# Attention scores that contract over all 128 rows, and value panels at twelve places

## The chip, the cores and the metric

The kernel runs on one core of a Trainium2 chip. The metric is the device time of one execution in microseconds (us). Engines are named as in the profile: PE is TensorE (matrix products; PEld are its weight loads), DVE is VectorE, ACT is ScalarE, POOL is GpSimd, SP is SyncE, which issues most transfers. TensorE takes a stationary operand (the weights, loaded first) and streams a moving operand; both have the contracted dimension on the partitions, of which there are 128.

## The reference, cut to what matters

Two transformer-like blocks, one after the other, each of two layers, on 256 tokens of width 1024. The first block also carries 256 context tokens. In each of its layers there are a feed-forward net, a mixing stage and another feed-forward net; the mixing stage has four branches: a Fourier mix, a neighbourhood attention (4 heads of 64), a gated linear attention, and a grouped-query attention (4 query heads on 2 key heads of 64). The second block has a latent attention (8 heads of 96), a differential attention, a memory attention and a squared-ReLU net. The scores that the change touches are these:

```
# neighbourhood attention: per head, 64 contracted channels, keys of the grid and of the context
s = concat([einsum(q, k_window) * scale + bias, einsum(q, k_ctx) * scale]);  p = softmax(s)
# grouped-query attention: two query heads share one key head
s = einsum('bqhgd,bkhd->bhgqk', q_blk, k);  p = softmax(s);  o = einsum(p, v)
# differential attention: two score maps of 64 channels for each head
o = softmax(q1 @ k1.T) @ v - lambda * softmax(q2 @ k2.T) @ v
```

## The kernel before, in words

Everything is kept with channels on the partitions and tokens along the rows of memory. A linear layer takes a weight panel of 1024 x 256 in two loads of 512 KB (`raw_panel`, line 118 on), splits each into a high and a low part of a shorter f32 format (`split`: ScalarE line 133, VectorE line 134) and forms three products for each 128 contracted channels (`mm3`). All products are issued in `mm`, line 84, so the profile shows that line for all of them and tells them apart by their tiles. In `lin_T` the panel is the stationary operand and the activations move; in `lin_tok` (line 190) it is the other way round: the panel moves. That form makes the values of the attentions: `gvt` and `nvt` in the first block, `dv` (line 1281) and the memory values (`mem_values`, line 303) in the second.

A split panel lies in a tile of 2112 words, and `off` (line 145) says at which word it begins; the low part follows 1024 words later. The panels of dv and of the memory values use `MOVING2 = 0`.

Scores are made by `scores` (line 249): products into a bank of TensorE's output memory, the row maximum (line 268), the exponential with its sum (line 272); `weights` divides by the sum and `transposed` (line 280) turns the weights for the product with the values.

In the neighbourhood attention (`na`, line 831) two heads lie in one tile, 64 channels each on partitions 0 to 63 and 64 to 127. A score product takes the 64 partitions of its head from the query tile `nq` and from the key tile `nk`. The grouped attention (`gqa`, line 910) does the same with the tile `gqt`, whose third part holds both key heads. These products are in full f32, which the trace shows as two passes for each. Keys and queries are normalized by `headnorm` (line 566): a copy out of the bank, a square, a product with a block matrix that gives the mean of each head's squares, and a scaling; `later` puts the second half of that behind the next product.

In the differential attention (`prepare`, line 1289, and `attend`, line 1362) each head pair has a query tile `a` (trace: `qs`) and a key tile `b_` (`ks`) of 128 partitions. For the map c, partitions of map c hold the high part of query and key, the other 64 the low part of the query beside a copy of the high part of the key. One product over 128 partitions so gives high x high and low x high. The tile `lk` holds the low part of the keys, and a second product, over the 64 partitions of map c alone, adds high x low:

```
scores([((a[:, c, j, w], b_[:, c, j]), (a[64 * c:64 * c + 64, c, j, w], lk[64 * c:64 * c + 64, j]))
        for j in range(2)], mp, after=after) for c in range(2)
```

`prepare` makes these tiles for one pair of heads with ScalarE (line 1297), VectorE (line 1298) and transfers on SP's queue (line 1302); it is called one pair ahead.

The order of the work is set in three ways. The calls give a program order; a planner then orders the instructions of each engine by that order and by when it expects their inputs, before the kernel runs; and `behind` adds edges by hand. In the mixing stage the branches are generators called in `ORDER` (line 44). In the differential attention `FILL` (line 60) says how many pieces of gate and merge products stand before and after the scores of each of the eight units (one unit is one pair of heads and 128 queries).

Of the kernel before, what the change touches and what calls it, by code (L numbers as in the profile page):

```python
# [13 lines left out]
F32 = mybir.dt.float32  # L14
# [63 lines left out]
def _build(ctx, nc, tc, A, out, tap, upto):  # L78
# [63 lines left out]

    WIDE, NARROW, MOVING, MOVING2 = 8, 24, 36, 0
    LATE = 28

    def panel(*srcs, off=WIDE):
# [153 lines left out]

    def mem_values(l, M, t0, dst):
        for c in range(2):
            pn = panel(A["mem_w_kv_2"][l][:, 512 + c * 256:768 + c * 256], off=MOVING2)
            ps = PM("pmv")
            for tb in range(2):
                lin_tok(ps[:, tb * 256:tb * 256 + 256], pn, cols(0, 256), M, t0 + tb * P)
            act(out=r2(dst).rearrange("p (t c) n -> p t c n", c=2)[:, :, c], in_=r2(ps), func=AF.Copy)
# [73 lines left out]

    slab = lambda name, dt=F32: mp.tile([P, 512], dt, name=name, tag="slab", bufs=10)
    gslab = lambda name, dt=F32: mp.tile([P, 512], dt, name=name, tag="gslab", bufs=10)
    tmp = lambda name="t": mp.tile([P, 512], F32, name=name, tag="tmp", bufs=3)

    def mixing_constants(after):
# [174 lines left out]
                    norm if g1 == NFF else None, side)  # L563


    def headnorm(raw, n, gain, dst, tiles=None, tag="po"):


        if raw is not None:
            act(out=dst, in_=raw, func=AF.Copy)  # L570
        sq, *tiles = tiles or [tmp("sqh"), *rs_tiles(mp)]
        sq = sq[:, :n]
        act(out=sq, in_=dst, func=AF.Square)

        def rest():
            pq = PM("phn", tag)
            after = newest[0]
            behind(mm(pq[:, :n], C["b64"], sq, start=True, stop=True), after)
            y = rstd(pq[:, :n], tiles)
            V.scalar_tensor_tensor(out=dst, in0=dst, scalar=gain, in1=y, op0=ALU.mult, op1=ALU.mult)  # L580
        return rest

    def mixing(l, H, first, last, side=None):
        W = A["w_in"][l]
# [215 lines left out]
        def na_in():  # L800

            pan = wpan("na_q")
            nq, nk = [], []
            for j in range(2):
                ps = PM("pnq")
                lin_T(ps[:, :nT], pan, cols(j * P, j * P + P), H, 0, nT)
                o = slab("nq")
                later(headnorm(ps[:, :nT], nT, gv[:, l, 0:1], o[:, :nT]))
                nq.append(o)
            yield  # L810
            pan = wpan("na_k")
            for j in range(2):
                ps = PM("pnk")
                lin_T(ps, pan, cols(j * P, j * P + P), H, 0, 512)
                o = slab("nk")
                later(headnorm(ps, 512, gv[:, l, 1:2], o))
                nk.append(o)
            yield
            pan = wpan("na_v")
            nvt = []  # L820
            for t in range(2):
                ps = PM("pnv")
                for b in range(2):
                    lin_tok(ps[:, b * 256:(b + 1) * 256], pan, cols(0, 256), H, (2 * t + b) * P)
                    later()
                o = slab("nvt")
                act(out=o, in_=ps, func=AF.Copy)
                nvt.append(o)
            T.nq, T.nk, T.na_v = nq, nk, lambda b, h: nvt[b // 2][:, (b % 2) * 256 + 64 * h:(b % 2) * 256 + 64 * h + 64]

        def na():

            nq, nk, na_v = T.nq, T.nk, T.na_v
            new_out(slab, 2, 3)
            for hp in range(2):
                bts = []
                for j in range(2):
                    bt = mp.tile([P, 512], F32, name="rpb", tag="rpb", bufs=2)
                    behind(nc.sync.dma_start(out=bt.rearrange("p (b k) -> p b k", b=2), in_=A["rpb"][l, 2 * hp + j]),
                           loaded[-1])  # L840
                    bts.append(bt)
                for qb in range(2):
                    w = slice(qb * P, qb * P + P)
                    pts = []
                    for j in range(2):
                        r = slice(64 * j, 64 * j + 64)
                        pts.append(weights([(nq[hp][r, w], nk[hp][r, :])], mp, bts[j][:, qb * 256:(qb + 1) * 256]))
                    po = PM("po", "po")[:, :P]
                    for b in range(4):
                        for j in range(2):  # L850
                            ins = mm(po[64 * j:64 * j + 64], na_v(b, 2 * hp + j), pts[j][:, b * P:(b + 1) * P], start=b == 0,
                                     stop=b == 3)
                    flow.append(ins)
                    put(2 + hp, w, po)
                    yield
            for qb in range(2 if zq else 0):
                w = slice(256 + qb * P, 256 + qb * P + P)
                pts = []
                for j in range(2):
                    r = slice(64 * j, 64 * j + 64)  # L860
                    pts.append(weights([(nq[c][r, w], nk[c][r, 256:]) for c in range(2)], mp))
                po = PM("po", "po")[:, :256]
                for c in range(2):
                    for b in range(2):
                        for j in range(2):
                            ins = mm(po[64 * j:64 * j + 64, c * P:c * P + P], na_v(2 + b, 2 * c + j),
                                     pts[j][:, (2 * c + b) * P:(2 * c + b + 1) * P], start=b == 0, stop=b == 1)
                flow.append(ins)
                for c in range(2):
                    put(2 + c, w, po[:, c * P:c * P + P])  # L870
                yield

        def gqa_in():

            gqt = mp.tile([P, 3, 512], F32, name="gqt", tag="gqt", bufs=1)
            pan = panel(A["w_gq"][l], off=NARROW if last else WIDE)
            for j in range(2):
                ps = PM("pqq")
# [4 lines left out]
            ps = PM("pqk")  # L883
            lin_T(ps, pan, cols(0, P), H, 0, 512)
            headnorm(ps, 512, gv[:, l, 3:4], gqt[:, 2, :])()
            ps = PM("pqv")
            lin_T(ps, pan, cols(P, 2 * P), H, 0, 512)
            later()
# [9 lines left out]
            for c, m in ((0, 2), (2, 1)):  # L898
# [6 lines left out]
                V.tensor_tensor(out=rot, in0=rot, in1=bc(ax[:, 256:]), op=ALU.mult)  # L905
                V.tensor_tensor(out=g, in0=g, in1=bc(ax[:, :256]), op=ALU.mult)
                V.tensor_tensor(out=g, in0=g, in1=rot, op=ALU.add)
            T.gqt, T.qv = gqt, qv

        def gqa():  # L910

            gqt, qv = T.gqt, T.qv
            new_out(slab, 6, 7)
            for kv in range(2):
                r = slice(64 * kv, 64 * kv + 64)
                for z in range(2 if zq else 1):
                    for qb in range(2):
                        w = slice(256 * z + qb * P, 256 * z + qb * P + P)
                        if z == 0:
                            pts = [weights([(gqt[r, c, w], gqt[r, 2, :])], mp) for c in range(2)]  # L920
                            at = lambda c, b: pts[c][:, b * P:(b + 1) * P]
                        else:
                            pt = weights([(gqt[r, c, w], gqt[r, 2, 256:]) for c in range(2)], mp)
                            at = lambda c, b: pt[:, (2 * c + b) * P:(2 * c + b + 1) * P]
                        po = PM("po", "po")[:, :P]
                        nb = 4 - 2 * z
# [120 lines left out]
    def _block2(c2):  # L1047
# [9 lines left out]
        x2 = lambda dp: x_all[:, 2 * dp:2 * dp + 2]  # L1057
        mean = {n: mp.tile([P, P], F32, name=f"mean{n}") for n in (384, 256)}
        mean[128] = C["b64"]
        for n, t in mean.items():  # L1060
            V.memset(t, 1.0 / n)

# [115 lines left out]
        for l in range(DEPTH):  # L1178
# [99 lines left out]
                    nc.gpsimd.dma_start(out=rotz[a:a + 8], in_=t[b:b + 8])  # L1278
                rope(t, rotz, cd, sd, slice(0, P), 8)
            for c in range(4):  # L1280
                pn = panel(W[:, OFF2["dv"] + 256 * c:OFF2["dv"] + 256 * c + 256], off=MOVING2)
                ps = PM("pdv")
                for tb in range(2):
                    lin_tok(ps[:, tb * 256:tb * 256 + 256], pn, cols(0, 256), X, tb * P)
# [4 lines left out]
            def prepare(hp):  # L1289
# [1 line left out]

                hs = slice(2 * hp, 2 * hp + 2)
                a, b_ = (med(n, F32R).rearrange("p (c h t) -> p c h t", c=2, h=2) for n in ("qs", "ks"))
                lk = mp.tile([P, 2, 256], F32R, name="lk", tag="lk", bufs=2)
                lq = r2(mp.tile([P, 512], F32R, name="lq", tag="tmp", bufs=5))
                for t, src, lo in ((b_, dk, lk), (a, dq, lq)):
                    act(out=t, in_=src[:, hs].unsqueeze(1).to_broadcast([P, 2, 2, 256]), func=AF.Copy)
                    V.tensor_tensor(out=lo, in0=src[:, hs], in1=t[:, 0].bitcast(F32), op=ALU.subtract)
                    for c in range(2):
                        own, other = (slice(64 * i, 64 * i + 64) for i in (c, 1 - c))  # L1300
                        part = t[own, c] if src is dk else lo[own]
                        nc.sync.dma_start(out=t[other, c].bitcast(F32), in_=part.bitcast(F32))
                return a, b_, lk
# [58 lines left out]
            def attend(u, after=None):  # L1362

                hp, qb = divmod(u, 2)
                if qb == 0 and hp < 3:
# [1 line left out]
                a, b_, lk = ready[hp]  # L1367
                w = slice(qb * P, qb * P + P)
                (p0, r0, _), (p1, r1, _) = (
                    scores([((a[:, c, j, w], b_[:, c, j]), (a[64 * c:64 * c + 64, c, j, w], lk[64 * c:64 * c + 64, j]))  # L1370
                            for j in range(2)], mp, after=after) for c in range(2))
                for j in range(2):
                    u, v_ = p0[:, 256 * j:256 * j + 256], p1[:, 256 * j:256 * j + 256]
# [352 lines left out]
```

## Time and profile before

| | us |
|---|---|
| median of 3 runs | 2816.1 (2815.95 to 2817.97) |
| the profiled execution | 2818.12 |
| its span, first to last instruction | 2816.3 |
| TensorE busy | 2766.3 |
| VectorE busy | 1930.4 |
| ScalarE busy | 1322.4 |
| GpSimd busy | 81.7 |

The span is what the trace covers; the profiled execution's own time is 1.8 us longer. Busy time of TensorE is the union of its matmuls' bars. The bars overlap, because matmuls are pipelined, so the distance from one start to the next says how long one takes in a stream, not the length of the bar. A row of the timeline merges equal neighbours: "x24" are 24 instructions, the second number is the time from the start of the first to the end of the last. "64*128" in a matmul's row are the contracted rows and the columns of its weights.

### The profile page before, as it was taken

Reading aid. Unit: us, or ns where it says so; the run is one execution under the profiler, and the core shown is the slowest. Engines: PE = TensorE matmul, PEld = TensorE weight load, DVE = VectorE, ACT = ScalarE, POOL = GpSimd, SP = SyncE. Lnnn points to the kernel's source line nnn. Section 1 sums busy time; section 2 is a strip of 40 time slices with the busy share of each in tenths; the row PEclk is TensorE's granted clock in tenths of the full one; section 3 lists DMA queues with packets and bytes.
Section 4 is the critical chain, followed back from the end, with each engine's and each line's share of the span. In section 5 each row is a group of like instructions: output and inputs, shape, how many; then the busy total and the mean of one; then the engine's idle time right before and its main releaser. Section 6 shows DMA issues by size and latency. Waiting matters only on the chain.

```text
span 2816.3 us, 45494 instructions
## 1 busy us (share of the span) xinstructions
PE 2766.3 (98%) x18310; PEld 2422.0 (86%) x18310; DVE 1930.4 (69%) x3049; ACT 1322.4 (47%) x2102; POOL 81.7 (3%) x93
## 2 busy tenths in 40 slices
PE   7999999999999999999999999999999999999998
PEld 4888887669888898888877999999899999999898
DVE  4978565856767568883568766576686576757766
ACT  5222245654323243232457644556755456566554
POOL 0000000000000000000000000000110011001100
PEclk9999999999999999999999999999999999999999
DMA  7766433114555436653333566647456655554564
GB/s 250 230 188 201 138 96 90 29 46 127 183 154 187 134 124 191 199 182 94 96 90 87 154 193 185 174 117 189 134 168 209 193 162 139 161 165 142 166 196 126
DMA packets 373735, 428.68 MB, mean 152 GB/s; under 512 B 17058, under 2 KB 351842, under 8 KB 373332
## 3 DMA queue, kind: packets, MB, share of 16 engines
q1 hardware_dynamic: 372036, 422.86, 49.7%
q0 software_dynamic: 1488, 2.90, 0.5%
q8 instruction: 144, 2.36, 0.4%
q14 instruction: 67, 0.55, 0.1%
HBM read 418.03 MB, written 1.06 MB: 149 GB/s over the span
## 4 chain that ended last, share of the span: by engine, by line
PE 89%; DVE 5%; ACT 3%; DMA 1%; issue 1%; SPq 0%; ACTq 0%; DVEq 0%
PE y L84 16%; PE u L84 15%; PE v L84 15%; PE pm L84 12%; PE pga L84 5%; PE s L84 4%; PE pdq L84 2%; PE pdv L84 2%; PE pt L280 1%; PE pbd L84 1%; PE po L84 1%; DVE whl L134 1%; ACT whl L133 1%; PE pnk L84 1%; PE pl L84 1%
## 5 line engine op out<-in xcount | busy, mean ns | idle before, releaser
L134 DVE TENSOR_TENSOR whl<-w,whl 128x1024 fp32r<-128x1024 f32 (+1 forms) x634 | 761.8, 1206 | 462.6 <-ACT whl L133 459.7
L133 ACT ACTIVATE whl<-w 128x1024 fp32r<-128x1024 f32 (+1 forms) x634 | 661.4, 1045 | 748.7 <-PE y L84 239.2
L84 PE MATMUL v<-hh,whl 128*128 128x512 f32 (+1 forms) x1472 | 397.0, 353 | 0.6 <-ACT whl L133 0.5
L84 PE MATMUL y<-gh,whl 128*128 128x512 f32 (+1 forms) x1552 | 394.5, 343 | 0.0
L84 PE MATMUL u<-hh,whl 128*128 128x512 f32 (+1 forms) x1344 | 374.6, 360 | 3.8 <-ACT hh L138 3.5
L84 PEld LDWEIGHTS y<-gh,whl 128*128 128x128 f32 x1552 | 268.8, 188 | 36.1
L84 PEld LDWEIGHTS v<-hh,whl 128*128 128x128 f32 x1472 | 260.0, 188 | 41.4 <-issue 1.6
L84 PEld LDWEIGHTS u<-hh,whl 128*128 128x128 f32 x1344 | 240.3, 188 | 44.8 <-ACT hh L138 3.7
L84 PE MATMUL y<-gl,whl 128*128 128x512 f32 (+1 forms) x776 | 266.0, 343 | 0.2 <-DVE gl L134 0.2
L84 PE MATMUL v<-hl,whl 128*128 128x512 f32 (+1 forms) x736 | 259.6, 353 | 0.0
L84 PE MATMUL u<-hl,whl 128*128 128x512 f32 (+1 forms) x672 | 243.1, 362 | 0.2
L1521 DVE SCALAR_TENSOR_TENSOR dot<-w,dot 128x1024 f32<-128x1024 f32 x172 | 210.3, 1223 | 18.9 <-DMA w<-in_w_modT 15.7
L84 PE MATMUL pm<-xhl,whl 128*128 128x256 f32 x1536 | 178.7, 277 | 5.7 <-ACT xhl L138 4.4
L84 PEld LDWEIGHTS pm<-xhl,whl 128*128 128x128 f32 x1536 | 176.7, 189 | 7.3 <-ACT xhl L138 5.1
L84 PE MATMUL pm<-gh,whl 128*128 128x256 f32 x1024 | 176.8, 276 | 0.4 <-ACT gh L133 0.4
L84 PEld LDWEIGHTS y<-gl,whl 128*128 128x128 f32 x776 | 146.0, 188 | 18.2 <-DVE gl L134 0.4
L84 PEld LDWEIGHTS pm<-gh,whl 128*128 128x128 f32 x1024 | 155.1, 188 | 0.9 <-ACT gh L133 0.8
L84 PEld LDWEIGHTS v<-hl,whl 128*128 128x128 f32 x736 | 138.2, 188 | 20.4 <-issue 1.2
L84 PEld LDWEIGHTS u<-hl,whl 128*128 128x128 f32 x672 | 126.2, 188 | 24.1 <-issue 2.9
L133 ACT ACTIVATE gh<-th 128x512 fp32r<-128x512 f32 (+1 forms) x88 | 50.8, 579 | 191.7 <-DVE th L549 191.4
L84 PE MATMUL pm<-gl,whl 128*128 128x256 f32 x512 | 140.8, 275 | 0.0
L84 PE MATMUL pga<-xhl,whl 128*128 128x256 f32 x1152 | 137.9, 278 | 0.0
(467 smaller groups left out, 4549.0 us busy)
## 6 DMA issues: line engine op xcount, KB each, us to landing
w<-in_ffn_w SPq DMA_DIRECT2D x240, 512.0 KB, 4.4
w<-in_w_in SPq DMA_DIRECT2D x144, 512.0 KB, 4.3
w<-in_mlp_w SPq DMA_DIRECT2D x128, 512.0 KB, 4.2
w<-in_w_modT SPq DMA_DIRECT2D x86, 512.0 KB, 3.4
dot<-in_w_modT SPq DMA_DIRECT2D x42, 512.0 KB, 4.5
w<-in_w_out SPq DMA_DIRECT2D x32, 512.0 KB, 4.0
w<-in_w_branch SPq DMA_DIRECT2D x32, 512.0 KB, 3.5
w<-in_ffn_w SPq DMA_DIRECT2D x32, 384.0 KB, 3.1
```

Source lines behind the costliest of these rows:

```text
L84: newest[0] = nc.tensor.matmul(*args, **kw)
L133: act(out=hi, in_=src, func=AF.Copy)
L134: V.tensor_tensor(out=lo, in0=src, in1=hi.bitcast(F32), op=ALU.subtract)
L280: newest[0] = nc.tensor.transpose(pt[:, b * P:(b + 1) * P], p[:, b * P:(b + 1) * P], C["ident"])
L1521: V.scalar_tensor_tensor(out=c2[2], in0=w, scalar=0.5, in1=c2[i], op0=ALU.mult, op1=ALU.mult, accum_out=mods[l][:, f, i:i + 1])
```

## The change

Scores of 64 contracted rows get 128. The query side takes all 128 partitions. The key side becomes one tile per head (or per map) in which the other head's 64 partitions are zero, so that the products are the same sums with zeros added.

- Neighbourhood attention: two key tiles per head pair, one in the slots of before and one in a new group of three slots (`nslab`). `heads_apart` clears the other half of each on GpSimd; `headnorm` with `apart` copies and scales each head's 64 partitions into its own tile and takes the square from the bank instead of from the copy.
- Grouped attention: two key tiles in `nslab` slots. The keys are normalized and rotated in `gqt` as before and then copied, 64 partitions at a time: the context half after the norm, the other after the rotation.
- Differential attention: two tiles `lk0` and `lk1`, allocated and half cleared once at the block's start, of twice the size, with the low part of map c on the partitions of c and zero elsewhere. VectorE fills them in two halves, each ahead of the transfer of that half.
- Value panels: `MOVING2` becomes a list of twelve places, one for each panel of the memory values (2 for each layer) and of dv (4 for each layer).

```diff
-    WIDE, NARROW, MOVING, MOVING2 = 8, 24, 36, 0
+    WIDE, NARROW, MOVING = 8, 24, 36
+    MOVING2 = (4, 12, 16, 20, 24, 28, 32, 40, 44, 48, 52, 56)
...
-            pn = panel(A["mem_w_kv_2"][l][:, 512 + c * 256:768 + c * 256], off=MOVING2)
+            pn = panel(A["mem_w_kv_2"][l][:, 512 + c * 256:768 + c * 256], off=MOVING2[2 * l + c])
...
+    nslab = lambda name, dt=F32: mp.tile([P, 512], dt, name=name, tag="nslab", bufs=3)
...
-    def headnorm(raw, n, gain, dst, tiles=None, tag="po"):
+    def headnorm(raw, n, gain, dst, tiles=None, tag="po", apart=None):
+        parts = [(slice(64 * j, 64 * j + 64), t) for j, t in enumerate(apart)] if apart else [(slice(0, P), dst)]
         if raw is not None:
-            act(out=dst, in_=raw, func=AF.Copy)
+            for r, d in parts:
+                act(out=d[r], in_=raw[r], func=AF.Copy)
...
-        act(out=sq, in_=dst, func=AF.Square)
+        act(out=sq, in_=raw if apart else dst, func=AF.Square)
...
-            V.scalar_tensor_tensor(out=dst, in0=dst, scalar=gain, in1=y, op0=ALU.mult, op1=ALU.mult)
+            for r, d in parts:
+                V.scalar_tensor_tensor(out=d[r], in0=d[r], scalar=gain[r], in1=y[r], op0=ALU.mult, op1=ALU.mult)
...
+    def heads_apart(*ts):
+        for j, t in enumerate(ts):
+            nc.gpsimd.memset(t[64 - 64 * j:128 - 64 * j], 0.0)
+        return ts
...
-                o = slab("nk")
-                later(headnorm(ps, 512, gv[:, l, 1:2], o))
-                nk.append(o)
+                nk.append(heads_apart(slab("nk"), nslab("nk")))
+                later(headnorm(ps, 512, gv[:, l, 1:2], None, apart=nk[-1]))
...
-                        pts.append(weights([(nq[hp][r, w], nk[hp][r, :])], mp, bts[j][:, qb * 256:(qb + 1) * 256]))
+                        pts.append(weights([(nq[hp][:, w], nk[hp][j])], mp, bts[j][:, qb * 256:(qb + 1) * 256]))
...
+            gk = heads_apart(nslab("gkz"), nslab("gkz"))
...
+            for j in range(2):
+                r = slice(64 * j, 64 * j + 64)
+                V.tensor_copy(out=gk[j][r, 256:], in_=gqt[r, 2, 256:])
...
+            for j in range(2):
+                r = slice(64 * j, 64 * j + 64)
+                V.tensor_copy(out=gk[j][r, :256], in_=gqt[r, 2, :256])
...
-                            pts = [weights([(gqt[r, c, w], gqt[r, 2, :])], mp) for c in range(2)]
+                            pts = [weights([(gqt[:, c, w], gk[kv])], mp) for c in range(2)]
...
+        lks = [mp.tile([P, 2, 2, 256], F32R, name=f"lk{i}") for i in range(2)]
+        for t in lks:
+            for c in range(2):
+                nc.gpsimd.memset(t[64 - 64 * c:128 - 64 * c, c].bitcast(F32), 0.0)
...
-                pn = panel(W[:, OFF2["dv"] + 256 * c:OFF2["dv"] + 256 * c + 256], off=MOVING2)
+                pn = panel(W[:, OFF2["dv"] + 256 * c:OFF2["dv"] + 256 * c + 256], off=MOVING2[4 + 4 * l + c])
...
-                lk = mp.tile([P, 2, 256], F32R, name="lk", tag="lk", bufs=2)
+                lk = lks[hp % 2]
...
-                    V.tensor_tensor(out=lo, in0=src[:, hs], in1=t[:, 0].bitcast(F32), op=ALU.subtract)
+                    if src is dq:
+                        V.tensor_tensor(out=lo, in0=src[:, hs], in1=t[:, 0].bitcast(F32), op=ALU.subtract)
                     for c in range(2):
                         own, other = (slice(64 * i, 64 * i + 64) for i in (c, 1 - c))
+                        if src is dk:
+                            V.tensor_tensor(out=lo[own, c], in0=src[own, hs], in1=t[own, c].bitcast(F32), op=ALU.subtract)
...
-                    scores([((a[:, c, j, w], b_[:, c, j]), (a[64 * c:64 * c + 64, c, j, w], lk[64 * c:64 * c + 64, j]))
+                    scores([((a[:, c, j, w], b_[:, c, j]), (a[:, c, j, w], lk[:, c, j]))
```

The context rows of the neighbourhood attention (`nk[c][j][:, 256:]`) and of the grouped attention (`gk[kv][:, 256:]`) change in the same way.

## Rows read from the trace of the kernel before

**Rows 1.** Page, part 1: engine, busy us, share of the span, instructions.
```profile
PE 2766.3 (98%) x18310; PEld 2422.0 (86%) x18310; DVE 1930.4 (69%) x3049; ACT 1322.4 (47%) x2102; POOL 81.7 (3%) x93
```

**Rows 2.** Waits of TensorE, whole span: us in total, times, longest.
```profile
PE s L84 <- ACT p L272: 2.1, 3, 0.8
PE pbd L84 <- ACT dh L133: 1.5, 2, 0.7
```

**Rows 3.** Table of stretches: length, busy us per engine (instructions), granted clock, DMA share, GB/s.
```profile
474.00:512.00 38.00, 37.40 (x244) 23.33 (x244) 29.78 (x77) 24.43 (x63) 0.00 (x0) 1.00 0.15 42
1931.00:2041.00 110.00, 109.72 (x831) 99.37 (x830) 70.19 (x115) 76.03 (x155) 7.20 (x5) 1.00 0.55 154
...
1780.00:2812.00 1032.00, 1009.55 (x8271) 967.02 (x8269) 703.21 (x970) 590.14 (x963) 70.23 (x68) 1.00 0.55 161
```

**Rows 4.** Timeline of TensorE, differential attention: start, us, operation, count, [idle before].
```profile
1938.65 0.36 PE L84 MATMUL s<-ks,qs 128*128 128x256 f32 x1
1938.94 0.38 PE L84 MATMUL s<-lk,qs 64*128 64x256 f32 x1
...
1941.12 2.69 PE L84 MATMUL pga<-xhl,whl 128*128 128x256 f32 x21
```

**Rows 5.** Timeline of TensorE, one stretch each of dv and of pm.
```profile
1901.46 23.20 PE L84 MATMUL pdv<-whl,xhl 128*128 128x256 f32 x192
...
2249.76 12.40 PE L84 MATMUL pm<-xhl,whl 128*128 128x256 f32 x108
```

**Rows 6.** Instructions of tile s: count, ns min/median/max, first and last start.
```profile
L84 PE MATMUL s<-lk,qs x64: 379/381/384, 1931.4 to 2551.9; 64*128 64x256 f32 x64
```

**Rows 7.** Timeline, second layer, preparation of the first heads.
```profile
2447.21 0.69 DVE L1298 TENSOR_TENSOR lk<-dk,ks 128x512 fp32r<-128x512 f32 x1 [0.29 <-ACT ks L1297]
...
2448.16 0.69 DVE L1298 TENSOR_TENSOR lq<-dq,qs 128x512 fp32r<-128x512 f32 x1 [0.26 <-ACT qs L1297]
...
2452.50 0.19 PEld L84 LDWEIGHTS s<-ks,qs 128*128 128x128 f32 x1 [0.42 <-issue]
```

**Rows 8.** Timeline of TensorE, neighbourhood attention.
```profile
483.61 0.60 PE L280 MATMUL pt<-cst,p 128*128 128x128 f32 x4
484.14 1.12 PE L84 MATMUL s<-nk,nq 64*128 64x512 f32 x2
485.20 0.70 PE L84 MATMUL pst<-gvt,kt 128*128 128x256 f32 x2
```

**Rows 9.** Timeline of TensorE, a 128-row f32 product between transposes.
```profile
575.58 0.38 PE L280 MATMUL pt<-cst,p 128*128 128x128 f32 x2
575.80 1.02 PE L84 MATMUL phn<-gn,cst 128*128 128x512 f32 x2
576.66 0.38 PE L280 MATMUL pt<-cst,p 128*128 128x128 f32 x2
```

**Rows 10.** Timeline of TensorE, the last run of f32 scores.
```profile
1545.90 1.12 PE L84 MATMUL s<-gqt 64*128 64x512 f32 x2
```

**Rows 11.** Timeline of TensorE, heads side by side.
```profile
478.78 1.13 PE L84 MATMUL s<-nk,nq 64*128 64x512 f32 x4
479.84 0.66 PE L671 MATMUL pkz<-cst,kz 128*128 128x128 f32 x4
...
482.03 1.12 PE L84 MATMUL s<-nk,nq 64*128 64x512 f32 x2 [0.60 <-ACT p L272]
...
500.13 1.13 PE L84 MATMUL s<-nk,nq 64*128 64x256 f32 x6
```

**Rows 12.** Instructions of tile nk, then timeline rows of the grouped keys.
```profile
L570 ACT ACTIVATE nk<-pnk x4: 597/597/599, 459.4 to 1447.6; 128x512 f32<-128x512 f32 x4
L580 DVE SCALAR_TENSOR_TENSOR nk<-nk,gv,rst x4: 750/752/752, 471.2 to 1457.0; 128x512 f32<-128x512 f32 x4
...
1522.39 0.42 DVE L907 TENSOR_TENSOR gqt<-gqt,rot 128x256 f32<-128x256 f32 x1
...
1523.06 1.98 PE L84 MATMUL s<-gqt 64*128 64x512 f32 x4
```

More of the change, by code (lines that the diff above doesn't have):

```diff
@@ L845, in na @@
                     for j in range(2):
-                        r = slice(64 * j, 64 * j + 64)
-                        pts.append(weights([(nq[hp][r, w], nk[hp][r, :])], mp, bts[j][:, qb * 256:(qb + 1) * 256]))
+                        pts.append(weights([(nq[hp][:, w], nk[hp][j])], mp, bts[j][:, qb * 256:(qb + 1) * 256]))
                     po = PM("po", "po")[:, :P]
@@ L859, in na @@
                 for j in range(2):
-                    r = slice(64 * j, 64 * j + 64)
-                    pts.append(weights([(nq[c][r, w], nk[c][r, 256:]) for c in range(2)], mp))
+                    pts.append(weights([(nq[c][:, w], nk[c][j][:, 256:]) for c in range(2)], mp))
                 po = PM("po", "po")[:, :256]
@@ L907, in gqa_in @@
                 V.tensor_tensor(out=g, in0=g, in1=rot, op=ALU.add)
-            T.gqt, T.qv = gqt, qv
+            for j in range(2):
+                r = slice(64 * j, 64 * j + 64)
+                V.tensor_copy(out=gk[j][r, :256], in_=gqt[r, 2, :256])
+            T.gqt, T.gk, T.qv = gqt, gk, qv
         def gqa():
-            gqt, qv = T.gqt, T.qv
+            gqt, gk, qv = T.gqt, T.gk, T.qv
             new_out(slab, 6, 7)
             for kv in range(2):
-                r = slice(64 * kv, 64 * kv + 64)
                 for z in range(2 if zq else 1):
@@ L919, in gqa @@
                         if z == 0:
-                            pts = [weights([(gqt[r, c, w], gqt[r, 2, :])], mp) for c in range(2)]
+                            pts = [weights([(gqt[:, c, w], gk[kv])], mp) for c in range(2)]
                             at = lambda c, b: pts[c][:, b * P:(b + 1) * P]
                         else:
-                            pt = weights([(gqt[r, c, w], gqt[r, 2, 256:]) for c in range(2)], mp)
+                            pt = weights([(gqt[:, c, w], gk[kv][:, 256:]) for c in range(2)], mp)
                             at = lambda c, b: pt[:, (2 * c + b) * P:(2 * c + b + 1) * P]
```

## The prediction

> **What bounds the kernel now.** I read the page's busy shares first: TensorE is busy for 2766.3 of 2816.3 us [rows 1]. Then its waits over the whole span: the attention stages appear there with no more than 2.1 us (scores) and 1.5 us (after the last attention unit) [rows 2]. So an edit is worth what it takes off TensorE's own sequence, and the question is how that sequence spends its time where scores are computed. The table of stretches says that TensorE is busy for 109.72 of 110 us in the second block's differential attention and 37.40 of 38 us in the neighbourhood attention, both at the granted clock 1.00, the upper level of 2.4 GHz, while VectorE and ScalarE have a fifth to a third of their time left [rows 3]. But busy is not streaming: a matmul's bar contains the wait for its weights. Therefore the next view is the timeline of TensorE, read by the distance between starts.
>
> **The change on TensorE, differential attention.** Each of these scores is a pair of products: 128 rows, then 64 rows, into the same bank. A run of eight begins at 1938.65 and the next gate product at 1941.12, so eight take 2.47 us, 0.31 each [rows 4]. The same shape among its like takes (12.40 - 0.28) / 107 = 0.113 us [rows 5]. The reader is to see that the bar lasts 0.38 instead of 0.28 and that no start falls before the previous product has left the array: the weights of a 64-row product are not loaded beside a 128-row product, nor the other way round, and each of the eight switches costs 0.2 us. With 128 rows on both sides there is no switch. I take 0.115 per product (a fresh run starts a little above 0.113) plus 0.09 at the first, which follows transposes now as later: 8 x 0.115 + 0.09 = 1.01 us instead of 2.47, and the gate product behind it loses its own 0.10. One run gives 1.56 us. The trace has 64 of the 64-row products [rows 6], four in a run, so 16 runs: 16 x 1.56 = **25.0 us**. What would be late next: inside the units TensorE has 2.5 panels of gate work between scores and transposes, and the scores themselves come earlier by the same amount. Only at the last units does the softmax chain show in the waits (the 1.5 us of rows 2); that is a rival below.
>
> **Preparing those scores.** The low part of the keys is now subtracted in two halves of 64 rows. VectorE's time goes with columns, so I count each half as the whole does today, 0.69 us [rows 7]: 8 x 0.69 = 5.5 us more VectorE, hidden under TensorE in a stage where VectorE works 70 of 110 us [rows 3], except for the first pair of heads of each layer. There the query's low part stands behind it on VectorE, then its transfer, then the first score, for which TensorE waits already in the second layer (0.42 us of weight loads, start 2452.50) [rows 7]. The subtraction would move from 2448.16 to 2448.6, and the weight panels' splits behind it on VectorE by up to 1.4. I take 0.5 a layer, **1.0 us** lost; ends 0 (if other products are put ahead of the score) and 2.8 (all 1.4 in both layers). The transfers of the key's high part no longer wait for that subtraction to have read their target, which can only help. The four clears at the block's start are GpSimd's, once, with nothing behind them that is due soon: 0.
>
> **Neighbourhood and grouped attention in the first block.** These are full f32: two passes of 512 columns each. One between 128-row neighbours goes from 484.14 to 485.20, 1.06 us, and the four transposes ahead of it take 0.53 [rows 8]. A 128-row f32 product of the same 512 columns, between transposes, takes 0.86, and two transposes 0.22 [rows 9]. So the run itself is 0.20 longer (0.11 at its first pass, 0.09 after its last), and the transposes ahead 0.53 instead of 0.44. A switch in front costs 0.09 + 0.11 = 0.20, one behind 0.09 and the late start of what follows, 0.20 in all for a wide product and 0.15 for transposes. Where the neighbour writes only 64 columns of the array (the value products), the switch stays whatever the scores do: the last such run stands at 1545.90 between two of them and saves nothing [rows 10]. I counted the neighbours of the 31 runs that don't run side by side, from 482.03 to 1545.90: 20 have a full neighbour in front, 11 a wide one behind, 15 transposes behind. 20 x 0.20 + 11 x 0.20 + 15 x 0.15 = 8.4 us.
>
> Against it stands what the 64 rows buy. Three times two heads' products lie side by side on the two halves of the array: at 478.78 four passes take 1.06 us where one after the other they will take 4 x 0.43 = 1.72, and the same in the second layer; six passes of 256 columns at 500.13 take 1.13 [rows 11], against 6 x 0.215 = 1.29 later. After the switches saved, the first two cost 0.50 each, the third 0.24: 1.2 us. Some of it disappears in the 0.60 us that TensorE waits at 482.03 anyway [rows 11]. Net 7.2 us.
>
> The Trainium skill, "TensorE: Matmul & The Clock Gate", section "Why this matters for your kernels", speaks against the change: products with few contracted rows should lie on distinct row groups, so that they run at once. By that rule all 12 pairs of heads in the neighbourhood attention would lose 0.50 us, 6 us instead of 1.2, and the whole sum would be some 5 us smaller. The rows show three such pairs; elsewhere other work stands between the two products, or both lie on the same rows.
>
> **What the first block pays.** The two key products of each layer are copied and scaled in halves: ScalarE +0.60 and VectorE +0.75 each [rows 12], four times. Hidden: the first layer's second key is scaled at 471.2 + 0.75 and the first score starts at 478.78 [rows 11]; in the second layer the value products stand between as well. The square reads the bank instead of the copy and holds it some 1.2 us longer; three banks rotate and the value products are next, so 0, at most 1.2 for each of four if they were not. The grouped keys get eight copies of 64 x 256, of which no row shows one; I bound each by 0 and the 0.42 us of a 128 x 256 two-operand product [rows 12], and take 0.25. Two of them per layer lie between the last rotation and the first score: in the second layer that is 1522.39 + 0.42 against 1523.06 [rows 12], so 0.5 us can show there unless another product fills it. The last cleared key tile takes over a slot of the neighbourhood keys and must wait for that attention to end; it is due twenty microseconds later. The softmax chain in the neighbourhood stage has VectorE at 29.8 of 38 us [rows 3], so not everything saved there arrives: of 7.2 I count **6.0 us**; ends 0 and 8.4.
>
> **The value panels.** 384 products in dv and 192 in the memory values stream a panel that begins at place 0: (23.20 - 0.28) / 191 = 0.120 us each, against 0.113 for the same shape [rows 5]. So the place of the moving operand is worth up to 0.0067 x 576 = 3.8 us. The twelve new places are not in the trace; the ends are 3.8 gained (all like the 0.113 row) and 3.8 lost (as much again on top of 0.120). I take half of the way to the better row, **1.9 us** gained.
>
> **Sum.** -25.0 + 1.0 - 6.0 - 1.9 = -31.9 us. The profiled execution took 2818.1 us (span 2816.3): 2786.2 for it, and since the median of the runs is 2 us lower, 2784.2 us as a median.
>
> **Rivals.**
> 1. *The softmax chain takes the place of the switches.* Scores come earlier, but what VectorE and ScalarE do with them doesn't get faster. For: waits at the end of the differential attention and at 482.03, VectorE at 78% in the neighbourhood stage. Against: in six of the eight units ten microseconds of gate products lie between. If the last two units of each layer give nothing (4 x 1.56 = 6.2) and the first block nothing (6.0): 2796.4.
> 2. *The change doesn't remove the switches,* because they come from something else than the row count, for instance from reading the same weights twice or from the bank. Against: 128-row products run into each other without a gap, f32 ones among f32r too [rows 9]. Then only panels (-1.9), preparation (+1.0) and pairs (+1.2) count: 2816.4.
> 3. *Slower: the new tiles move every other tile.* The key tiles with zeros stand at the head of the second block's memory. Rows 5 show that the place of an operand decides between 0.113 and 0.120. If all later tiles came to a bad place, most of 8271 products from 1780 to 2812 [rows 3] would take 0.0067 us more, 55 us: 2839. It decides from 4,800 products on (31.9 / 0.0067). Against: what is added is 2 x 4096 and 3 x 2048 bytes, so places modulo 256 stay.
>
> **How the numbers follow.** Forecast 0.76, rival 1 0.16, rival 2 0.05, rival 3 0.03. The forecast's own terms reach from 2776 (panels at their best, all of the first block, nothing lost in preparation, and 2 us of what a shifted order of instructions may do) to some 2790; with rival 1 the range goes to 2798. Beyond it lie rivals 2 and 3 and a little on either side. About 0.2% (5.6 us) is what a measurement of this kernel can tell from no change: faster 0.92 (forecast and rival 1), same 0.05, slower 0.03.
>
> **What would show it.** Right: scores of the differential attention start 0.113 to 0.12 us apart and a run of eight takes 1.0 us; the first product behind them takes 0.11; runs of f32 scores between transposes take 0.86; no two heads' scores overlap; the differential stage of each layer is 12 us shorter, with TensorE still busy throughout. Wrong: gaps of TensorE ahead of the transposes that wait for VectorE or ScalarE (rival 1), score bars of 0.38 us (rival 2), gate and MLP products at 0.120 (rival 3). A first score of a layer that starts more than 1 us later than its transfer allows would show the preparation mis-sized, and dv products that still take 0.120 the panels.

## The result, and the profile after

The changed kernel takes 2787.31 us (median of 4 runs, 2786.48 to 2789.8) beside 2816.62 (4 runs, 2815.95 to 2817.97): ratio 0.9897, interval 0.9885 to 0.991, 29.3 us less. The forecast was 2784.2 in 2776 to 2798. Measured once more (experiment 11), the same two kernels took 2785.66 and 2817.08 (ratio 0.9889, 0.9874 to 0.9904), 31.4 us less; so a difference of 1 to 2 us between two medians here says little, and small terms are read from the traces.

The profiled execution of the changed kernel took 2789.8 us, span 2788.0. Its busy times:

```profile
PE 2737.5 (98%) x18310; PEld 2416.3 (87%) x18310; DVE 1938.3 (70%) x3069; ACT 1321.2 (47%) x2106; POOL 90.1 (3%) x109
```

Against [rows 1], TensorE has the same 18310 products and is busy for 28.8 us less, while the span is 28.3 us shorter (2816.3 to 2788.0); VectorE has 7.9 us more. So it was time inside TensorE's bars that went. Its waits over the whole span, as in [rows 2] (us in total, times, longest):

```profile
PE pt L281 <- DVE p L1398: 1.6, 3, 0.5
PE pbd L84 <- ACT dh L133: 1.5, 2, 0.8
...
PE s L84 <- ACT p L273: 0.5, 1, 0.5
PE s L84 <- issue: 0.4, 1, 0.4
```

The first line is new: transposes wait for VectorE's last step between the exponential and the transposes. The scores' wait of 2.1 us has shrunk to 0.5. The stretches of [rows 3], shifted to where they now lie:

```profile
474.00:512.00 38.00, 38.00 (x259) 26.07 (x258) 31.42 (x79) 25.89 (x66) 0.98 (x2) 1.00 0.15 45
1925.50:2025.50 100.00, 99.10 (x837) 96.41 (x837) 72.36 (x120) 75.54 (x157) 7.42 (x6) 1.00 0.60 175
1774.00:2783.00 1009.00, 985.29 (x8271) 959.11 (x8269) 706.51 (x976) 586.62 (x962) 72.44 (x72) 1.00 0.56 165
```

The first two stretches are the ones to read: 259 instead of 244 products in the same 38 us, and 837 in 100 us where 831 took 110. The granted clock stays 1.00. In the second, TensorE now has 0.9 us without work, where it had 0.3. One run of scores in the differential attention, which answers to [rows 4]:

```profile
1931.52 0.44 PE L281 MATMUL pt<-cst,p 128*128 128x128 f32 x2
1931.71 0.37 PE L84 MATMUL s<-ks,qs 128*128 128x256 f32 x1
1931.92 0.28 PE L84 MATMUL s<-lk,qs 128*128 128x256 f32 x1
1932.04 0.28 PE L84 MATMUL s<-ks,qs 128*128 128x256 f32 x1
...
1932.65 0.28 PE L84 MATMUL s<-lk,qs 128*128 128x256 f32 x1
1932.77 2.54 PE L84 MATMUL pga<-xhl,whl 128*128 128x256 f32 x21
1935.15 1.05 PE L84 MATMUL pdo<-pts,dv 128*128 128x128 f32 x8
```

Read by starts: the run takes 1932.77 - 1931.71 = 1.06 us instead of 2.47, its products start 0.12 apart, and the 21 gate products behind it (1935.15 - 1932.77) / 21 = 0.113 each, the first included. The bar of a low product is 0.28 instead of 0.38. What the longer bar holds is the load of the weights (PEld). The second product of a run, in the kernel before and then in the changed one:

```profile
1931.40 0.18 PEld L84 LDWEIGHTS s<-lk,qs 64*128 64x128 f32 x1
1931.40 0.38 PE L84 MATMUL s<-lk,qs 64*128 64x256 f32 x1
...
1931.80 0.19 PEld L84 LDWEIGHTS s<-lk,qs 128*128 128x128 f32 x1
1931.92 0.28 PE L84 MATMUL s<-lk,qs 128*128 128x256 f32 x1
```

The load began together with its product before; now it begins 0.12 us ahead of it, beside the product in front, which started at 1931.71. The neighbourhood attention, which answers to [rows 8] and [rows 11]:

```profile
479.81 1.88 PE L84 MATMUL s<-nk,nq 128*128 128x512 f32 x4
481.52 0.60 PE L682 MATMUL pkz<-cst,kz 128*128 128x128 f32 x4
...
484.36 0.60 PE L281 MATMUL pt<-cst,p 128*128 128x128 f32 x4
484.80 1.02 PE L84 MATMUL s<-nk,nq 128*128 128x512 f32 x2
485.66 0.59 PE L84 MATMUL pst<-gvt,kt 128*128 128x256 f32 x2
```

Two passes now take 0.86 us instead of 1.06, and the transposes ahead of them 0.44 instead of 0.53; the four passes that ran side by side in 1.06 us take 1.71, one after the other. The dv products, first and second layer, beside [rows 5]:

```profile
1895.45 23.00 PE L84 MATMUL pdv<-whl,xhl 128*128 128x256 f32 x192
...
2405.14 22.95 PE L84 MATMUL pdv<-whl,xhl 128*128 128x256 f32 x192
```

That is (23.00 - 0.28) / 191 = 0.119 us each, hardly less than the 0.120 of before. Last, where the first row of the waits stands, in the last unit of the first layer:

```profile
2016.86 1.52 PE L84 MATMUL pbm<-memo,whl 128*128 128x256 f32 x12
2018.89 0.74 PE L281 MATMUL pt<-cst,p 128*128 128x128 f32 x4 [0.51 <-DVE p L1398]
```

### The profile page after: what moved, and what is told of

Same layout as the page of the kernel before. It is cut to its first block, busy times and chain, and to the rows that moved or that the text cites. A ratio compares the mean times of both kernels' runs of the same rounds, so it can differ in the third digit from the quotient of the medians.

```text
span 2788.0 us, 45556 instructions
## 1 busy us (share of the span) xinstructions
PE 2737.5 (98%) x18310; PEld 2416.3 (87%) x18310; DVE 1938.3 (70%) x3069; ACT 1321.2 (47%) x2106; POOL 90.1 (3%) x109
## 3 DMA queue, kind: packets, MB, share of 16 engines
HBM read 418.03 MB, written 1.06 MB: 150 GB/s over the span
## 4 chain that ended last, share of the span: by engine, by line
PE 87%; DVE 6%; ACT 4%; DMA 1%; issue 1%; SPq 0%; ACTq 0%; DVEq 0%
PE y L84 16%; PE u L84 15%; PE v L84 15%; PE pm L84 12%; PE pga L84 4%; PE s L84 3%; PE pdq L84 2%; PE pdv L84 2%; PE pt L281 1%; DVE whl L134 1%; PE pbd L84 1%; PE po L84 1%; ACT whl L133 1%; PE pnk L84 1%; PE pl L84 1%
```

## The experiments

**1. The differential attention alone.** The kernel before with the zero-filled low keys of the second block and nothing else (of the edit, the line of the scores):

```diff
...
-(a[64 * c:64 * c + 64, c, j, w], lk[64 * c:64 * c + 64, j])
+(a[:, c, j, w], lk[:, c, j])
```

> The kernel before with the differential attention's part of the change alone: zero-filled low keys, all eight score products over 128 rows. Theory (switches of row count cost 0.2 us each): scores 0.113 to 0.13 us apart, a run of eight 1.0 us, 16 runs x 1.56 = 25 us less on TensorE, of which the trace of the changed kernel shows 22 to 23 arriving, so about 2794. Rival 1 (the softmax chain takes their place): the saving would be 19 us or less, 2797 or more. Rival 2 (the gap comes from something else than the row count): 2816 to 2817.

2794.77 us against 2816.41 (ratio 0.9923, 0.9908 to 0.9937): 21.6 less. The order of the products, their banks and the repeated reading of the weights are as before, and the extra time goes with the 64 rows, so the rival that it comes from elsewhere falls; the rival of the softmax chain holds for a small part, since transposes wait for VectorE 1.7 us in all, four times.

**2. The first block alone.** The changed kernel with the differential attention's part undone and the value panels back at place 0 (two of the edit's places):

```diff
-MOVING2 = (4, 12, 16, 20, 24, 28, 32, 40, 44, 48, 52, 56)
+MOVING2 = (0,) * 12
...
-(a[:, c, j, w], lk[:, c, j])
+(a[64 * c:64 * c + 64, c, j, w], lk[64 * c:64 * c + 64, j])
```

> The changed kernel with the differential attention and the twelve value panels put back, so that only the first block's neighbourhood and grouped scores contract over 128 rows. Theory: 6 to 7 us less than before, about 2810; together with the run of the differential part alone and 1 us of the panels the three add up to the change's 29.3 us. Rival (the first block's softmax chain keeps what is saved): 2815 to 2817, and the two parts would not add up.

2809.84 us (ratio 0.9975, 0.9965 to 0.9986): 6.6 less. With 21.6 and some 1 us of the panels (counted from the trace, under *Value panels* below) the parts add up to 29.2.

**3. Fewer switches, the same 64 rows.** The kernel before with the eight products of two banks in another order: two of 128 rows, two of 64, twice (the lines that set up the banks and the order by hand are left out).

```diff
+for j in range(2):
+    for t in range(2):
+        for c in range(2):
+            r = slice(64 * c, 64 * c + 64)
+            x, y = (a[r, c, j, w], lk[r, j]) if t else (a[:, c, j, w], b_[:, c, j])
+            ins = mm(banks[c][:, 256 * j:256 * j + 256], x, y, start=t == 0, stop=t == 1)
```

> The kernel before, 64-row low products kept, but the eight products of two banks are issued as two of 128 rows, two of 64, two of 128, two of 64: four switches in a run instead of eight, the same products, banks and weights. Theory (each switch costs 0.2 us): 16 x 4 x 0.2 = 12.8 us less, and 16 x 2 x 0.1 = 3.2 more if the two neighbouring 64-row products, which lie on different halves of the rows, run at once: 2801 to 2804. If it is the low product's reading of the same weights right after the high one, or its adding into the same bank right behind it, the cause is gone in all eight: about 2791. If every 64-row product is slow by itself: 2816.

2803.38 us (ratio 0.9953, 0.9938 to 0.9968): 13.0 less. The timeline of one run:

```profile
1936.59 0.48 PE L84 MATMUL s<-ks,qs 128*128 128x256 f32 x2
1937.00 0.39 PE L84 MATMUL s<-lk,qs 64*128 64x256 f32 x2
1937.32 0.50 PE L84 MATMUL s<-ks,qs 128*128 128x256 f32 x2
1937.75 0.38 PE L84 MATMUL s<-lk,qs 64*128 64x256 f32 x2
1938.06 2.13 PE L84 MATMUL pga<-xhl,whl 128*128 128x256 f32 x16
```

The run takes 1.47 us, 1.00 less than in [rows 4]: four switches of 0.2, and 0.1 twice because the two 64-row products lie on different halves of the rows and run at once (a pair's bar is 0.39, one alone has 0.38). So the 64-row products are not slow by themselves: same weights, same banks, same 64-row products, and the time goes with the number of switches. Sixteen such runs would save 16.0 us. The 13.0 fit, because the first unit of each layer kept the old order, with gate products between its two banks, and gave nothing (7.46 and 7.54 us to the second unit before, 7.45 and 7.54 now), and a transpose in each last unit now waits 0.5 us for VectorE. The Trainium skill, "TensorEngine Tiling (Array Packing)", section "Key Properties", says that a change of the tiling mode drains the engine; the trace agrees, with 0.2 us for each change.

**4. All value panels at one place.**

```diff
-MOVING2 = (4, 12, 16, 20, 24, 28, 32, 40, 44, 48, 52, 56)
+MOVING2 = (20,) * 12
```

> The changed kernel with all twelve value panels at place 20, at which the trace of the changed kernel has one memory panel at 114 ns from start to start where the twelve lie between 114 and 120. If the place alone decides, all 576 products of pdv and pmv come to 0.113 to 0.114 us: 384 x 0.0049 + 192 x 0.0035 = 2.5 us less than the changed kernel, about 2785. If the tile or the layer decides, dv products stay near 0.118 and the time within 0.7 us of the changed kernel.

2784.7 us against 2816.41 (ratio 0.9886, 0.9872 to 0.9901): 31.7 less, where the change has 29.3 and 31.4. The dv products of either layer:

```profile
1893.60 21.93 PE L84 MATMUL pdv<-whl,xhl 128*128 128x256 f32 x192
...
2401.58 21.93 PE L84 MATMUL pdv<-whl,xhl 128*128 128x256 f32 x192
```

(21.93 - 0.28) / 191 = 0.1134 us each: the place decides, not the tile or the layer, and all of the 1.3 us a layer that [rows 5] promised can be had.

**5. Twelve other places.**

```diff
+MOVING2 = (8, 36, 60, 0, 18, 19, 21, 22, 2, 6, 14, 30)
```

> The changed kernel with the value panels at twelve other places: 8, 36, 60, 0 (memory values), 18, 19, 21, 22, 2, 6, 14, 30 (dv). If the pitch is the place's own, 18 to 22 lie at 113 to 115 ns, 0 at 120.0 as before, and the places by 32 apart are alike; if only place 20 is good, the neighbours lie at 118 to 120.

A single run took 2787.16 us. The expectation's first case failed; nearer to its second, only place 20 is good. Read by starts, panel by panel, dv lies at 117 ns (place 19), 120 to 122 (18, 21, 22, 2, 6, 14, 30), the memory values at 118 to 120; place 0 has 120 again. The first three dv panels (places 18, 19 and 21, 47 of the 48 products of each), then both layers' rows:

```profile
1892.72 5.88 PE L84 MATMUL pdv<-whl,xhl 128*128 128x256 f32 x47
1898.44 5.67 PE L84 MATMUL pdv<-whl,xhl 128*128 128x256 f32 x47
1904.18 5.80 PE L84 MATMUL pdv<-whl,xhl 128*128 128x256 f32 x47
...
1892.60 23.19 PE L84 MATMUL pdv<-whl,xhl 128*128 128x256 f32 x192
...
2402.13 23.27 PE L84 MATMUL pdv<-whl,xhl 128*128 128x256 f32 x192
```

**6. The query prepared first.** In `prepare`, on the changed kernel:

```diff
-for t, src, lo in ((b_, dk, lk), (a, dq, lq)):
+for t, src, lo in ((a, dq, lq), (b_, dk, lk)):
```

> The changed kernel with the query's high and low parts of each pair of heads prepared ahead of the key's. If the 0.4 to 0.6 us that the first score waits in the first layer comes from the key's halved subtraction standing ahead of the query's on VectorE, that wait goes: about 0.6 us less than the changed kernel's 2787.3, and nothing elsewhere. If the first score waits for something else (the key's transfer, a bank), or the key comes as much later as the query comes earlier: 0, or some tenths more.

2786.72 us against 2816.0 (ratio 0.9897, 0.9881 to 0.9914), no gain that can be told. In the first layer the wait is gone, in the second there is one of 0.83 us where the changed kernel has none:

```profile
2430.23 0.35 PE L84 MATMUL s<-ks,qs 128*128 128x256 f32 x1 [0.83 <-ACT whl L133]
```

The planner put 46 gate products ahead of the first score instead of 59, so the cover moved with the order; what the preparation costs by itself stays open within 1 us.

**7. One more panel under the last unit's softmax.**

```diff
-FILL = (..., (1, 2, (0,)), (0, 1, (1,)), (1, 0, (2,)))
+FILL = (..., (1, 1, (0,)), (0, 2, (1,)), (1, 0, (2,)))
```

> The changed kernel with one panel of other work moved from behind the scores of the seventh unit to behind those of the eighth, the last. If the softmax chain took back what the switches gave in the last unit (0.51 us ahead of its transposes and 0.30 ahead of its value products, in each layer), those waits go and the time falls by 1.0 to 1.6 us, unless the seventh unit, now with the shorter cover, begins to wait by the same amount: then 0.

2785.58 us against 2816.0 (ratio 0.9892, 0.9878 to 0.9907): 30.4 less. The medians don't tell it from the change, the trace does:

```profile
2014.90 1.53 PE L84 MATMUL pbm<-memo,whl 128*128 128x256 f32 x12
2016.27 0.60 PE L281 MATMUL pt<-cst,p 128*128 128x128 f32 x4
...
2030.85 0.50 PE L84 MATMUL pbd<-dh,whl 128*128 128x256 f32 x2 [0.95 <-DVE whl L134]
```

No transpose of this stage waits any more, in either layer, and the differential stage (first score to first product behind the stage) is 103.9 us in both layers instead of 104.6 and 105.2: 2.0 us in all. But 0.5 of that only moved: in the second layer the first score now waits 0.34 us and comes 0.5 later behind the first gate product (7.23 instead of 6.72), and the first unit's transposes wait no more. Counted from the first gate product it is 111.16 us in both layers instead of 111.95 and 111.90, 1.5 us in all, within the 1.0 to 1.6 expected. The next product group then waits 0.95 instead of 0.8, and for VectorE's split of its weights, not for the attention's last output. So the wait in the last unit was the softmax chain with too little work beside it.

**8. Neighbourhood heads side by side.** The changed kernel with 64-row neighbourhood scores, both heads issued together behind the value products of the pair before (the lines that issue a pair):

```diff
+for i, c in enumerate(cs):
+    for j in range(2):
+        r, n = slice(64 * j, 64 * j + 64), keys.stop - keys.start
+        ins = mm(banks[j][:, i * n:i * n + n], nq[c][r, w], nk[c][r, keys], start=True, stop=True)
+        if i == j == 0 and flow[-1:]:
+            behind(ins, flow[-1])
```

> The changed kernel with the neighbourhood attention back on 64 rows per head, but with both heads' products issued back to back on the two halves of the rows, each such pair behind the value products of the pair before. Theory of the row halves (the page's rule for few contracted rows): ten pairs of four passes take 1.06 us instead of two runs of 0.86, so 0.66 less each, less 0.2 for the switch behind: 4 to 5 us less on TensorE, about 2783, and less the rest if the later start of each softmax chain is covered by the keys' and gates' products. If that chain is not covered: 2787 or more, with gaps of TensorE ahead of the transposes. If the halves don't run at once: two products take 2 x 0.86 + 0.2 and the time rises by some 2 us.

2791.43 us against 2816.0 (ratio 0.9915, 0.99 to 0.9929): 24.6 less, where the change has 29.3 and 31.4. A pair in the timeline, and three stretches of this kernel (columns as in [rows 3]):

```profile
488.30 1.13 PE L84 MATMUL s<-nk,nq 64*128 64x512 f32 x4
489.36 1.12 PE L84 MATMUL pl<-qm,dl 128*128 128x512 f32 x2
```

```profile
474.00:512.00 38.00, 36.72 (x254) 24.70 (x253) 28.99 (x69) 22.28 (x48) 0.00 (x0) 1.00 0.21 56
512.00:560.00 48.00, 47.27 (x372) 31.94 (x371) 37.73 (x97) 34.91 (x77) 0.00 (x0) 1.00 0.08 23
560.00:620.00 60.00, 57.25 (x372) 39.69 (x371) 43.84 (x95) 38.70 (x87) 4.78 (x9) 1.00 0.20 60
```

The first of these stretches stands above for the changed kernel (38.00 busy); its other two:

```profile
512.00:560.00 48.00, 47.93 (x367) 32.20 (x366) 39.16 (x94) 31.50 (x59) 4.17 (x8) 1.00 0.14 42
560.00:620.00 60.00, 60.00 (x382) 41.55 (x381) 42.07 (x92) 38.22 (x88) 1.04 (x2) 1.00 0.17 53
```

The pairs do run at once, four passes in 1.06 us; what is saved is lost because TensorE stands idle for 4.8 us in these stretches instead of 0.07; 2.8 of it is the wait of the first grouped score for its keys. Why, is argued and not tested: each pair starts only behind the value products of the pair before, so each softmax chain begins later. The planner's order also moved: 37 of the 48 products of the first layer's grouped queries (`pqq`) now start before 505 us, where the changed kernel has 4, so they are gone as cover later on. The Trainium skill's rule that products with few contracted rows should share the array ("TensorE: Matmul & The Clock Gate", section "Why this matters for your kernels") agrees with the pair's 1.06 us, but not with the time of this kernel. Whether an order exists that keeps both wasn't tried.

**9 to 11. The edits together, and the change again.** Experiments 4, 6 and 7 in one kernel, then 4 and 7 beside the changed kernel on one chip:

> The changed kernel with the value panels at place 20, the query prepared first and the panel moved to the last unit: -2.6 us as measured for the panels, -0.6 and -1.0 to -1.6 if the two other expectations hold and add up: about 2782.5 to 2783.5; 2784.7 if neither holds.

> The changed kernel with the value panels at place 20 and the panel moved to the last unit, the key prepared first as in the change: -2.6 us for the panels and -1.0 to -1.7 for the moved panel, if they add up: about 2783, and 1 to 2 us less than with the query first, whose trace shows a first score that waits 1.7 us. If they don't add up: 2784.5.

> The changed kernel itself once more, beside the two below: 2787, to compare with on the same chip, and a second profile of it.

All three: 2784.43 us against 2816.0 (ratio 0.9889, 0.9874 to 0.9904). Panels and fill: 2784.29 (2782.91 to 2786.78), and the change 2785.66 (2785.42 to 2787.64), against 2817.08 (ratios 0.9881, 0.9865 to 0.9898, and 0.9889). The best version is 1.4 us under the change, less than can be told, so the medians don't say whether the gains add up. The trace of panels and fill shows a place where a part is taken back, the first score of the second layer:

```profile
2424.78 6.86 PE L84 MATMUL pga<-xhl,whl 128*128 128x256 f32 x59
2432.92 0.35 PE L84 MATMUL s<-ks,qs 128*128 128x256 f32 x1 [1.28 <-DMA qs<-lq]
```

The dv products take 1.0 us less than in the changed kernel, the same 59 gate products follow, and then the first score waits for the transfer of the query's low part, which did not come earlier by as much (in experiment 4 it waits 0.9 there). From the first gate product to the first product behind the stage the second layer takes 111.80 us, where the changed kernel takes 111.90 and experiment 7 took 111.16: some 0.6 of the 1.0 that the panels save ahead of it comes back, because the chain of the preparation is there as long as the TensorE work that covers it. In the first layer it is 111.13, and nothing comes back.

## Why the prediction was right, point by point

*Differential attention (-25.0 forecast).* The mechanism and the size of a run were right: 2.47 to 1.06 us and the gate product behind at 0.113; from the second unit on, each unit of the first layer is 1.5 to 1.6 us shorter until the last (17.17 to 15.61 for the second interval between first scores). By stages, first score to the first product behind: -11.7 and -11.2 us, so the term was too large by 2.1. The softmax chain takes 0.51 and 0.53 in the last unit of each layer and 0.52 ahead of the first unit's transposes in the second layer: rival 1's mechanism, at a quarter of its price of 6.2, since a last unit gives up 0.5 of its 1.56 and not all. The count of 16 equal runs was wrong too: the first unit's scores come as two runs of four and gave 0.65 to 0.69 each in the first layer, not half of 1.56. And one reading does not hold in its words: in [rows 4] a start does fall before the bar ahead has ended (1938.94 against 1938.65 + 0.36 = 1939.01). What shows the switch is that a weight load does not begin ahead of its product.

*Preparation (+1.0).* The key's halves take 0.69 each, as forecast. The first layer's first score waits 0.41 and comes 0.6 later behind the gate's start, in the second layer the wait of [rows 7] is gone and it comes 0.4 earlier: +0.2 net.

```profile
1918.28 6.89 PE L84 MATMUL pga<-xhl,whl 128*128 128x256 f32 x59
1925.59 0.35 PE L84 MATMUL s<-ks,qs 128*128 128x256 f32 x1 [0.41 <-issue]
...
2427.93 6.89 PE L84 MATMUL pga<-xhl,whl 128*128 128x256 f32 x59
2434.65 0.33 PE L84 MATMUL s<-ks,qs 128*128 128x256 f32 x1
...
2440.77 0.44 PE L281 MATMUL pt<-cst,p 128*128 128x128 f32 x2 [0.52 <-DVE p L1398]
```

But this wait and the one ahead of the first unit's transposes can't be parted. From the gate's first product to the second unit's first score both layers take 13.43 us (13.42 and 13.43 in the second profile of the changed kernel), wherever the wait stands; without one it would be 6.69 + 6.12 = 12.81. VectorE, with the preparation, the panels' splits and the first softmax, has less than 1 us of gaps in that time. So each layer loses 0.6 there; the second lost 0.5 of it before too (14.64 us against 14.15 in the first). Taken together the change costs some 0.8 us, near the forecast 1.0; how much of it is the longer preparation and how much the softmax, no run shows.

*First block (-6.0).* Right in sum: 6.6 alone (experiment 2). By stages it is 4.6 in the first layer and 3.0 in the second, from the first neighbourhood score to the next feed-forward net; the serial pairs cost what was counted (1.71 us for four passes), and no wait for the softmax has grown there: the one of [rows 2] shrank from 2.1 to 0.5, so about all of the 7.2 arrived. The discount to 6.0 for VectorE's chain was not needed.

*Value panels (-1.9).* The step that failed: "half of the way to the better row". The twelve places differ: 114.0 ns for place 20, 116.6 for 12, 117.9 to 120.0 for the other ten. Against the 120.0 of before that is 0.97 us over 576 products. The bound was right (all at place 20: 0.113).

*The sum.* -22.9 + 0.2 - 7.6 - 1.0 = -31.3 by stages, beside the forecast -31.9. That the two are so close is in part luck: the differential attention and the panels gave 2.1 and 0.9 less than forecast, the first block and the preparation's own term were 1.6 and 0.8 better. The spans differ by 28.3 in this profile and by 30.4 with the second one of the changed kernel (span 2785.9). The two profiles of the one kernel are 1.7 us apart already at the first neighbourhood score (479.81 and 478.12; 478.78 before). So of the 3.1 us between forecast and median, 0.6 is in the terms. The rest lies outside their stages, where the first profile takes 3.0 us more than the kernel before and the second 1.0. Behind the last differential stage both profiles take 0.8 us more than before (248.2 instead of 247.4), which no run explains.

*Rivals.* Rival 1 held at the few places named above and gave 1.6 of its 12.2 us. Rivals 2 and 3 fell: score bars are 0.28, and gate products stay at 0.113.

## What to carry to other kernels

Read TensorE by the distance between starts: an engine that is busy for 98% can still lose time inside its bars, here 0.2 us at each change between 64 and 128 contracted rows, and zeros in unused rows take that away; an order that groups equal row counts takes away a part (13.0 instead of 21.6 us). When a busy engine gets faster, look for the chains that its work has covered with little to spare (here the last unit's softmax and the first unit's preparation): they give back the next microseconds. Two heads side by side gain only where both can start together without holding up the chain behind them.

## What the runs showed of the hardware that was not expected

The pitch of products with the value panel as moving operand depends on the panel's place to a single word: 113.4 ns at place 20, 117 at 19, 120 at 21, and 121.6 at 18, worse than the 120 at 0. Twenty-four places were looked at and one comes to 113 ns; whether it does so by itself or against the place of the stationary operand, which stayed where it was, is open. Two 64-row products on different halves of the rows and in different banks run at once in the shorter f32 format too, a pair in 0.3 us from its start to the next product's with the switch behind it included. Scores over 96 rows, which the latent attention has, show no switch: in the kernel before, eight passes of 256 columns take 1.64 us up to the next 128-row product (1841.06 to 1842.70), and four behind transposes 0.68 (1848.71 to 1849.39).
